# V rows of a scan step from 128-row products, and new cost estimates for a planner

## The chip, the cores and the metric

The kernel runs on one core of a Trainium2 chip. The time is the device time of one execution in microseconds, and the median of the runs is what is compared. TensorE (PE) does the matrix products, VectorE (DVE) and ScalarE (ACT) the elementwise work, GpSimd (POOL) a little of it, and SyncE (SP) issues the DMA transfers, in the order of its queue.

## The reference

One layer of a hybrid model on 512 latent and 128 context tokens of width 1024. Cut to what matters here:

```python
def _wkv(s0, r, w, k, v, a, b, reverse):
    def step(S, inp):
        rt, wt, kt, vt, at, bt = inp
        sa = jnp.einsum('bhvk,bhk->bhv', S, at)
        S = S * wt[:, :, None, :] + sa[..., None] * bt[:, :, None, :] + vt[..., None] * kt[:, :, None, :]
        return S, jnp.einsum('bhvk,bhk->bhv', S, rt)
    s_fin, ys = lax.scan(step, s0, xs, reverse=reverse)

def _layer(x, cond, s0_f, s0_b, rows, lp):
    mod = jax.nn.silu(cond) @ lp['ada_w'] + lp['ada_b']
    sh1, sc1, g1, sh2, sc2, g2 = jnp.split(mod[:, None, :], 6, axis=-1)
    xn = _rmsnorm(x, lp['norm1_g']) * (1 + sc1) + sh1
    proj = xn @ lp['w_in']                      # r, k, v, GLU input, two gates
    y_r, s_f, s_b = _rwkv_branch(xn, rkv, s0_f, s0_b, lp)   # _wkv in both directions, 8 heads of 64
    y_c = _conv_branch(glu_in, rows, lp)
    merged = jax.nn.sigmoid(gate_r) * y_r + jax.nn.sigmoid(gate_c) * y_c
    x = x + g1 * (merged @ lp['w_o'])
    xn2 = _rmsnorm(x, lp['norm2_g']) * (1 + sc2) + sh2
    x = x + g2 * (jnp.square(jax.nn.relu(xn2 @ lp['mlp_w1'])) @ lp['mlp_w2'])
```

All is computed in float32.

## The kernel before

Channels lie on the 128 partitions and the 640 tokens in the free dimension. A dense product in full precision is made of three products of split operands (`mm3`), 24 instructions of 128x128 by 320 columns for each half of four weight tiles. The kernel has three stages. First come the norm, the first 16 column blocks of the modulation `mod` and the low-rank products (to about 60 us). Then, to about 780 us, runs a mixed stage: the input projections, the scan, the convolution, the gates and the merge. Then follow the output projection and the MLP, dense work alone.

The scan works in chunks of 32 tokens. A head pair `p` (four of them, two heads `s` each, two directions `d`) has its own operands, its triangular solve (`solve`, with `gram`, `inverse` and `fold`) and its chain of 20 steps (`chain`). A step multiplies the state and the V rows, which lie stacked in the tile `svu`, by the chunk's operands. The V rows enter PSUM through `values`: four small products (two heads, two directions) with a part of an identity matrix move 32 tokens of V to the partitions where the chain needs them. `vS` holds V and `vr` holds V in reversed order. ACT then copies the sum of V rows and state products (the `ps` products of the step) into `svu`.

The order of PE, DVE and ACT in the mixed stage is written out by the program itself. Generators ("lanes") issue their instructions and yield: a number is a wait in planned us, a bare `yield` means to go on when the last issued instruction is done, by the plan, plus `SEM` (0.2), and a letter names an engine that has to be nearly free. The main loop takes the most urgent lane that is ready (`URGENT`), and fills PE with dense products where none is. The planned time `now` moves with PE's products (`mm`), and the functions `cost_v`, `cost_a` and `cost_g` estimate the other engines. `mm` also keeps an account of columns: a float32 product adds its cycles, times its rows / 128, times 0.5; the account drains with planned time at `QUOTA * ENTRY / TICK`, and while it is low (`hungry`) dense products go first. A wait that the plan does not know of, say for a transfer or for a PSUM bank, stands in PE's queue for real, and all products behind it wait too. SP's queue is not written out in this way.

The lane `ada_all` makes the other 32 column blocks of `mod`, which are read only behind the mixed stage. For each it waits `GAP_ADA`, then `ada` loads the first half of the weights (256 KB) into `adl`, which has one buffer, and issues its four products; waits 2.5; loads the second half into the same buffer, and issues four more. The loads come out of a generator (`adl_load`), so each is issued by the program right ahead of its products; SP may run it as soon as the buffer is read and all that stands before it in SP's queue is out.

`operands(p)` ends with two DVE operations on `kk`, whose result `bonus(p)` multiplies on PE. `inverse(p)` uses three DVE transposes of 128x1024. `root` raises a small tile to a power on GpSimd.

Of the kernel before, what the change touches and what calls it, by code (L numbers as in the profile page):

```python
# [13 lines left out]
ALU = mybir.AluOpType  # L14
# [46 lines left out]
LEAD, SEM, LOAD = 0.40, 0.2, 4.0  # L61
# [1 line left out]

URGENT = dict(scan=0, split=0.3, shift=1.45, post=1, side=0.9, solve=1, prep=1.5, lora=2, ada=4, out=4.5, branch=0.5, conv=1.6)

GAP_LORA, GAP_ADA = 1.5, 3.5
V_STEP = 20
GLU_AT = 12
TICK, ENTRY, QUOTA, CREDIT, STAY, DEBT = 3.413, 3060, 1.55, 700, 350, 6000
# [7 lines left out]
def hybrid_step(ctx: ExitStack, tc: tile.TileContext, I, O):  # L77
# [32 lines left out]
    def aps_(kw, *names):  # L110
        return sum(hasattr(kw.get(k), "shape") for k in names)

    def cost_v(name, n, src, kw):
        return 0.07 + 0.06 * aps_(kw, "scalar", "scalar1") + n / (480 if name == "tensor_tensor_scan" else 960)

    def cost_a(name, n, src, kw):
        return (0.08 if src[0].space == PSUM else 0.16) + 0.093 * aps_(kw, "scale", "bias") + n / 1400

    def cost_g(name, n, src, kw):
        return 1.9 if kw.get("op") == ALU.pow else 0.26 + n / (450 if name == "tensor_tensor" else 960)  # L120

    V, A, G = Timed(nc.vector, "V", cost_v), Timed(nc.scalar, "A", cost_a), Timed(nc.gpsimd, "G", cost_g)

    def advance(t):
        dt, now[0] = max(t - now[0], 0.0), max(now[0], t)
        gated["credit"] = max(gated["credit"] - QUOTA * ENTRY / TICK * dt, -DEBT)
        while now[0] >= gated["end"]:
            gated.update(cols=0.0, end=gated["end"] + TICK, warm=gated["cols"] >= ENTRY)

    def bank(tag="mm"):  # L130
        return pp.tile([P, 512], F32, name="ps_" + tag, tag=tag, bufs=2 if tag == "mm" else 1)
# [10 lines left out]
    def ldtmp():  # L142
        pool, n, cols = tmp_pool[-1]
        return pool.tile([P, cols], F32, name="tmp", tag="tmp", bufs=n)
# [10 lines left out]
    ident = cst[:, CST_ID:CST_ID + 128]  # L155
# [36 lines left out]
    def mm(out, lhsT, rhs, start=True, stop=True, **kw):  # L192
        PE.matmul(out=out, lhsT=lhsT, rhs=rhs, start=start, stop=stop, **kw)  # L193
        cyc = math.prod(rhs.shape[1:]) * (1 if rhs.dtype == F32R else 2 if "is_transpose" in kw else 4)
        m = math.prod(lhsT.shape[1:])
        overlap = 128 // m if m < 128 else 128 // rhs.shape[0]
        cols = cyc * rhs.shape[0] / 128 * (1 if rhs.dtype == F32R else 0.5)
        gated["cols"] += cols
        gated["burst"] -= cols
        gated["credit"] = min(gated["credit"] + cols, CREDIT)  # L200
        kind = (m, rhs.shape[0], rhs.dtype)
        if kind != gated["kind"]:
            advance(now[0] + SWITCH * gated["drain"] / (2400 if gated["warm"] else 1200))
        gated.update(kind=kind, drain=0 if rhs.dtype == F32R else max(cyc, 256) - max(cyc / overlap, 64))
        advance(now[0] + (max(cyc / overlap, 64) + EXTRA) / (2400 if gated["warm"] else 1200))
        ready[out.name] = ("P", now[0] + SEM / 2)
        last[0] = now[0]
# [7 lines left out]
    planner, calm = [lambda: None], []  # L215
# [167 lines left out]
    def ada(cols, tag, raws):  # L383

        n = len(cols) * P
        ps = bank(tag)
        for k0, k1, raw in raws:
            for k in range(k0, k1):
                g = 32 * (k % 4)
                mm(ps[g:g + 32, 0:n], csb[:, 2 * k:2 * k + 32], raw[:, k - k0, :], k < 4, k >= 4, tile_position=(0, g))  # L390
            yield 2.5 if k0 == 0 else 0.0
        e = ldtmp()[:, 0:n]
        A.activation(e, ps[:, 0:n], AF.Copy)
        yield
        for i, col in enumerate(cols):
            mm(ps[:, n + 2 * i:n + 2 * i + 2], e[:, i * P:(i + 1) * P], sel)
        for i, col in enumerate(cols):
            A.activation(mod[:, col, :], ps[:, n + 2 * i:n + 2 * i + 2], AF.Identity, bias=pc("ada_b", col))
# [52 lines left out]
    for k in range(KD):  # L451
        q = sut([P, T], "sq", 2) if k else sums
# [3 lines left out]
    ps = bank("t")  # L456
# [5 lines left out]
    for tag, a, b in (("a0", 0, 4), ("b0", 4, 5)):  # L462
        ps = bank(tag)
# [90 lines left out]
    rk, grp, shifting = {}, {}, []  # L554
# [107 lines left out]
    def operands(p):  # L662

        gr = grp[p]
        gr["Dc"] = wt([P, NY], "Dc", 2)
        r, k = rk[0, p], rk[1, p]

        def load(d):
            th, at = st([P, T], "tA"), st([P, T], f"ath{d}")
            DMA.dma_start(out=th, in_=dram(f"z0{d}{p}"))  # L670
            DMA.dma_start(out=at, in_=dram(f"z1{d}{p}"))
            return th, at

        loaded = load(0)
        t0 = st([P, T], "pt0")
        A.activation(t0, k, AF.Square, scale=pc("k_k", p))
        kk = gr["kk"] = st([P, T], "kk")
        yield
        yield from inv_norm(t0, 1.0, "max", 1e-24, ("t",) * 3,
                            lambda a, b, ps: V.scalar_tensor_tensor(out=kk[:, a:b], in0=k[:, a:b], scalar=pc("k_k", p),  # L680
                                                                    in1=ps, op0=ALU.mult, op1=ALU.mult))
        ath = []
        for d in range(2):
            ys = slice(20 * d, 20 * d + 20)

            def tv(ap):
                return (ap[:, ::-1] if d else ap).rearrange("p (y t) -> p y t", t=C32)


            th, at = loaded  # L690
            ath.append(at)
            A.activation(th, th, AF.Copy, bias=1.0)
            yield "T"
            cs = st([P, 20, C32], "tB")
            csf = cs.rearrange("p y t -> p (y t)")
            for a, b in HALVES:
                V.tensor_tensor_scan(out=csf[:, a:b], data0=smask, data1=th[:, a:b], initial=0.0,
                                     op0=ALU.mult, op1=ALU.add)
                yield "V"
            if d == 0:  # L700
                loaded = load(1)
            yield "T"
            A.activation(E[:, :, 1:33], cs, AF.Exp, scale=-0.5 * CDEC)
            yield "A"
            A.activation(cs, cs, AF.Exp, scale=0.5 * CDEC)
            yield "A"
            if d == 0:
                while p and (3 not in rates or (p > 1 and p - 2 not in chained)):
                    yield 0.2
                ARGH = gr["ARGH"] = st([P, 2, NY, 64], "ARGH", 2)  # L710
            A.activation(gr["Dc"][:, ys].unsqueeze(2), E[:, :, 32:33], AF.Copy)
            V.tensor_tensor(out=ARGH[:, 0, ys, 0:32], in0=tv(kk), in1=E[:, :, 0:32], op=ALU.mult)
            yield "V"
            V.tensor_tensor(out=ARGH[:, 0, ys, 32:64], in0=tv(r), in1=E[:, :, 1:33], op=ALU.mult)
            DMA.dma_start(out=ARGH[64:128, 1, ys, :], in_=ARGH[64:128, 0, ys, :])
            yield "V"
            if d == 0:
                while p and turned[p - 1] < 3:
                    yield 0.2
                BK = gr["BK"] = wt([P, NY, 64], "BK")  # L720
            bc, kc = (0, 32) if d == 0 else (32, 0)
            t1 = st([P, T], "pt0")
            V.scalar_tensor_tensor(out=t1, in0=at, scalar=1.0, in1=kk, op0=ALU.add, op1=ALU.mult)
            yield "V"
            V.scalar_tensor_tensor(out=BK[:, ys, bc:bc + 32], in0=tv(t1), scalar=-0.5, in1=cs,
                                   op0=ALU.mult, op1=ALU.mult)
            yield "A"
            A.activation(at, at, AF.Identity, scale=ka2[:, p:p + 1], bias=ka2[:, 4 + p:5 + p])
            yield "T"
            V.tensor_tensor(out=at, in0=at, in1=k, op=ALU.mult)  # L730
            yield "V"
            V.tensor_tensor(out=BK[:, ys, kc:kc + 32], in0=tv(at), in1=cs, op=ALU.mult)
            yield "V"
        operated.add(p)
        V.tensor_tensor(out=kk, in0=ath[0], in1=ath[1], op=ALU.add)
        yield "V"
        V.scalar_tensor_tensor(out=kk, in0=kk, scalar=pc("r_k", p), in1=r, op0=ALU.mult, op1=ALU.mult)
        yield SEM

    BKt = wt([P, 2, NY, 64], "BKt")  # L740
    for s in range(2):
# [3 lines left out]
    vr = wt([P, T], "vr")  # L745
# [14 lines left out]
    def vq(s, d):  # L760
        return 32 * (2 * (1 - s) + 1 - d)
# [218 lines left out]
    def cidx(c, i):  # L980

        return (i, 4 + i) if c == "l" else (16 + i, i)

    STEPS = [("c", i) for i in range(4)] + [("l", i) for i in range(16)]

    def values(p, n):

        S, ps = SVU[n % 2], grp[p]["ps"]
        for s, d in UNITS:
            lo, q, t = 64 * s, vq(s, d), 32 * cidx(*STEPS[n])[d]  # L990
            mm(ps[q:q + 32, d, :], (vr if d else rk[2, p])[lo:lo + 64, t:t + 32], ident[lo:lo + 64, lo:lo + 64],
               tile_position=(lo, q))
        for s in range(2):
            o = slice(64 - 64 * s, 128 - 64 * s)
            A.activation(S[o, :, s, :], ps[o], AF.Copy)
# [654 lines left out]
```

## Time and profile before

| | us |
|---|---|
| median of 3 runs | 1296.28 |
| lowest and highest | 1286.36, 1297.65 |
| profiled execution | 1300.42 |
| its span, first to last instruction | 1298.6 |

In the profiled execution PE is busy for 95% of the span, DVE for 56%, ACT for 42% and GpSimd for 12%; PE's mean granted clock is 0.958 of its full 2.4 GHz. The times of busy PE are modelled, as matmuls are pipelined, so the start-to-start distance of two groups says more than a duration. A wait is put down to what came last before the engine went on.

### The profile page before, as it was taken

To read this page: it belongs to the slowest core of one execution; us is meant where nothing else is said; L and a number is where in the kernel's file an instruction comes from. 1 tells how busy PE (TensorE), PEld (TensorE's weight loads), DVE (VectorE), ACT (ScalarE), POOL (GpSimd) and SP (SyncE) were. 2 spreads that over 40 slices of the span, in tenths; PEclk is the share of its full clock that TensorE was granted. 3 is DMA by queue.
4 is the path that set the end of the run, shared out by engine and by line. 5 is a ranking of instruction groups with operands and counts; after the bars stand their busy time and mean duration, and the time that the engine had idled before them with its cause. 6 is when DMAs were issued, how large, how long until landed. Compare 5 with 4: busy or idle time off the path is not lost.

```text
span 1298.6 us, 31716 instructions
## 1 busy us (share of the span) xinstructions
PE 1228.2 (95%) x13362; PEld 1092.9 (84%) x13362; DVE 720.9 (56%) x1446; ACT 548.8 (42%) x1390; POOL 152.4 (12%) x112
## 2 busy tenths in 40 slices
PE   8988899998999899999979999999999999999996
PEld 5776676777677776777979999999999999999996
DVE  5525576747557766877953365664433443444344
ACT  5545466634555565465225123354421431342130
POOL 1122120112011100122413310000000000000000
PEclk9998999968799989999989999999999999999998
DMA  9445433113222522343413853112222222222222
GB/s 370 151 158 175 143 109 114 59 43 119 77 94 68 153 92 70 116 126 93 136 58 121 270 195 125 49 50 82 72 75 81 67 82 74 74 82 69 78 74 82
DMA packets 82575, 140.43 MB, mean 108 GB/s; under 512 B 17024, under 2 KB 31616, under 8 KB 82432
## 3 DMA queue, kind: packets, MB, share of 16 engines
q1 hardware_dynamic: 82432, 138.39, 33.2%
q8 instruction: 105, 1.72, 0.6%
q14 instruction: 38, 0.31, 0.1%
HBM read 113.52 MB, written 22.22 MB: 105 GB/s over the span
## 4 chain that ended last, share of the span: by engine, by line
PE 82%; DVE 7%; DMA 6%; issue 2%; ACT 1%; SPq 0%; POOL 0%; POOLq 0%; DVEq 0%; ACTq 0%
PE ps_mm L193 43%; PE ps_b L193 24%; PE ps_t L193 7%; PE ps_a L193 6%; DMA adl_w<-in_adal 3%; PE ps_ad L193 3%; DVE BK_w L106 2%; DVE cacc_w L106 1%; DMA adar_s<-in_adaw 1%; DVE vS_w L106 1%; DVE ARGH_t L106 1%; DMA u_t<-gate 1%; DMA svu_w<-in_st 0%; DVE kk_t L106 0%; DVE svu_w L106 0%
## 5 line engine op out<-in xcount | busy, mean ns | idle before, releaser
L193 PE MATMUL ps_mm<-xh_t,wh_t 128*128 128x320 f32 x584 | 198.2, 339 | 0.9 <-ACT tmp L106 0.9
L193 PE MATMUL ps_mm<-xh_t,wl_t 128*128 128x320 f32 x584 | 198.8, 340 | 0.0
L193 PE MATMUL ps_mm<-xl_t,wh_t 128*128 128x320 f32 x584 | 196.7, 337 | 0.0
L106 ACT ACTIVATE wh_t<-wr_t 128x512 fp32r<-128x512 f32 x135 | 84.9, 629 | 143.2 <-PE ps_b L193 108.4
L106 POOL TENSOR_TENSOR wl_t<-wr_t,wh_t 128x512 fp32r<-128x512 f32 x63 | 85.0, 1350 | 462.0 <-ACT wh_t L106 418.0
L106 ACT ACTIVATE svu_w<-ps_a 64x128 f32<-64x128 f32 x320 | 87.0, 272 | 122.9 <-PE ps_a L193 117.3
L193 PEld LDWEIGHTS ps_mm<-xh_t,wl_t 128*128 128x128 f32 x584 | 117.0, 200 | 10.8 <-issue 7.2
L193 PEld LDWEIGHTS ps_mm<-xl_t,wh_t 128*128 128x128 f32 x584 | 116.7, 200 | 9.6 <-issue 6.1
L193 PEld LDWEIGHTS ps_mm<-xh_t,wh_t 128*128 128x128 f32 x584 | 116.3, 199 | 9.6 <-issue 4.3
L106 DVE SCALAR_TENSOR_TENSOR cacc_w<-upad_w,par_t,cacc_w 128x640 f32<-128x640 f32 x90 | 88.6, 984 | 4.3 <-ACT cacc_w L106 2.1
L106 DVE TENSOR_TENSOR wl_t<-wr_t,wh_t 128x512 fp32r<-128x512 f32 x72 | 49.7, 690 | 56.2 <-ACT wh_t L106 56.2
L106 ACT ACTIVATE tmp<-ps_mm 128x320 f32<-128x320 f32 x80 | 34.9, 436 | 98.9 <-PE ps_mm L193 90.4
L193 PE MATMUL ps_mm<-ARGH_t,wh_t 128*128 128x320 f32 x284 | 74.8, 308 | 0.0
L106 DVE TENSOR_TENSOR svu_w<-ps_b,Dc_w 64x128 f32<-64x128 f32 x152 | 43.7, 288 | 54.5 <-PE ps_b L193 51.0
L106 POOL TENSOR_TENSOR rt_t<-rt_t,mhalf_t 128x3 f32<-128x3 f32 (+1 forms) x7 | 6.5, 921 | 532.0 <-DVE rt_t L106 532.0
L193 PE MATMUL ps_mm<-ARGH_t,wl_t 128*128 128x320 f32 x212 | 65.8, 310 | 0.0
L106 ACT ACTIVATE mwh<-wr_t 128x512 fp32r<-128x512 f32 x49 | 31.0, 632 | 71.1 <-PE ps_b L193 66.8
L106 DVE SCALAR_TENSOR_TENSOR ARGH_t<-ps_mm,mod_t,ARGH_t 128x320 f32<-128x320 f32 (+2 forms) x45 | 22.6, 511 | 59.9 <-PE ps_mm L193 59.9
L106 DVE TENSOR_TENSOR tmp<-tmp 128x320 f32<-128x320 f32 x64 | 31.2, 489 | 43.8 <-ACT tmp L106 43.7
L106 DVE TENSOR_TENSOR mwl<-wr_t,mwh 128x512 fp32r<-128x512 f32 x49 | 33.8, 690 | 34.9 <-ACT mwh L106 34.9
L193 PEld LDWEIGHTS ps_mm<-ARGH_t,wh_t 128*128 128x128 f32 x284 | 50.4, 188 | 0.0
L106 ACT ACTIVATE BKt_w<-ps_a 32x512 f32<-32x512 f32 (+3 forms) x80 | 39.9, 503 | 19.9 <-PE ps_a L193 18.9
(372 smaller groups left out, 3226.2 us busy)
## 6 DMA issues: line engine op xcount, KB each, us to landing
wr_t<-in_w SPq DMA_DIRECT2D x214, 256.0 KB, 2.7
adl_w<-in_adal SPq DMA_DIRECT2D x64, 256.0 KB, 3.0
adar_s<-in_adaw SPq DMA_DIRECT2D x16, 512.0 KB, 8.4
ARGH_t<-in_x SPq DMA_DIRECT2D x8, 640.0 KB, 6.9
z<-tmp SPq DMA_DIRECT2D x32, 160.0 KB, 3.0
gate<-tmp SPq DMA_DIRECT2D x32, 160.0 KB, 2.2
tA_t<-z SPq DMA_DIRECT2D x8, 320.0 KB, 3.1
ath_t<-z SPq DMA_DIRECT2D x8, 320.0 KB, 3.3
```

Of the source, the lines that this page charges most:

```text
L106: return f(*args, **kw)
L193: PE.matmul(out=out, lhsT=lhsT, rhs=rhs, start=start, stop=stop, **kw)
```

## The change

The products of `values` read all 128 rows of V, with the 64 columns of the 128x128 identity that pick the head, in place of 64 rows with a 64x64 identity. They are the same four a step, with the same results. Five estimates of the plan are changed: the wait ahead of a modulation column (`GAP_ADA`) and between its halves, the cost of a DVE transpose, the cost of the power on GpSimd, and the end of `operands`, which now goes on when its last operation is done by the plan and not 0.2 us later.

```diff
-GAP_LORA, GAP_ADA = 1.5, 3.5
+GAP_LORA, GAP_ADA = 1.5, 4.5
     def cost_v(name, n, src, kw):
-        return 0.07 + 0.06 * aps_(kw, "scalar", "scalar1") + n / (480 if name == "tensor_tensor_scan" else 960)
+        return 0.07 + 0.06 * aps_(kw, "scalar", "scalar1") + n / (480 if name == "tensor_tensor_scan" else 520 if name == "transpose" else 960)
     def cost_g(name, n, src, kw):
-        return 1.9 if kw.get("op") == ALU.pow else 0.26 + n / (450 if name == "tensor_tensor" else 960)
+        return 2.6 if kw.get("op") == ALU.pow else 0.26 + n / (450 if name == "tensor_tensor" else 960)
     def ada(cols, tag, raws):
-            yield 2.5 if k0 == 0 else 0.0
+            yield (GAP_ADA if calm else 2.5) if k0 == 0 else 0.0
     def operands(p):
         V.scalar_tensor_tensor(out=kk, in0=kk, scalar=pc("r_k", p), in1=r, op0=ALU.mult, op1=ALU.mult)
-        yield SEM
+        yield
     def values(p, n):
         for s, d in UNITS:
-            lo, q, t = 64 * s, vq(s, d), 32 * cidx(*STEPS[n])[d]
-            mm(ps[q:q + 32, d, :], (vr if d else rk[2, p])[lo:lo + 64, t:t + 32], ident[lo:lo + 64, lo:lo + 64],
-               tile_position=(lo, q))
+            q, t = vq(s, d), 32 * cidx(*STEPS[n])[d]
+            mm(ps[q:q + 32, d, :], (vr if d else rk[2, p])[:, t:t + 32], ident[:, 64 * s:64 * s + 64], tile_position=(0, q))
```

`calm` is set in the mixed stage.

## Rows read from the trace of the kernel before

**Rows 1.** The page's part 2: granted clock in tenths, 40 slices

```profile
PEclk9998999968799989999989999999999999999998
```

**Rows 2.** Windows: stretch, length, busy PE, PEld, DVE, ACT, POOL, clock, DMA, GB/s

```profile
60.00:780.00 720.00, 667.41 (x9535) 549.52 (x9532) 448.46 (x886) 352.40 (x995) 140.45 (x99) 0.93 0.38 119
780.00:1298.60 518.60, 505.65 (x3452) 504.74 (x3450) 238.01 (x482) 165.27 (x323) 3.40 (x4) 0.99 0.24 76
```

**Rows 3.** Waits of PE: who waited for whom, us in total, times, longest

```profile
PE ps_ad L193 <- DMA adl_w<-in_adal: 17.0, 9, 2.9
PE ps_t L193 <- DVE kk_t L106: 7.5, 8, 1.8
...
PE ps_mm L193 <- DVE BK_w L106: 5.7, 2, 5.2
```

**Rows 4.** Timeline of PE, one step: start, us, operation, tile, count

```profile
448.21 0.32 PE L193 MATMUL ps_a<-svu_w,ARGH_t 128*32 128x64 f32 x8
448.46 0.43 PE L193 MATMUL ps_t<-ARGH_t,svu_w 128*64 128x32 f32 x8
...
449.66 0.45 PE L193 MATMUL ps_b<-svu_w,BKt_w 128*64 128x64 f32 x8
450.04 0.25 PE L193 MATMUL ps_a<-cst_t,vS_w 64*32 64x64 f32 x2
...
450.28 0.41 PE L193 MATMUL ps_mm<-xl_t,wh_t 128*128 128x320 f32 x1
```

**Rows 5.** Tile adl_w: products (ns min/median/max, first and last start), transfers' landing

```profile
L193 PE MATMUL ps_ad<-adl_w,csb_t x512: 272/297/423, 59.7 to 552.3; 128*32 128x128 f32 x171
...
DMA to landing us min/median/max: 2.5/3.0/5.0
```

**Rows 6.** Timeline of PE: the waits for adl_w over 2 us

```profile
64.72 0.43 PE L193 MATMUL ps_ad<-adl_w,csb_t 128*32 128x128 f32 x8 [2.07 <-DMA adl_w<-in_adal]
...
77.62 0.65 PE L193 MATMUL ps_ad<-adl_w,csb_t 128*32 128x128 f32 x8 [2.55 <-DMA adl_w<-in_adal]
...
112.01 0.65 PE L193 MATMUL ps_ad<-adl_w,csb_t 128*32 128x128 f32 x8 [2.29 <-DMA adl_w<-in_adal]
...
328.03 0.66 PE L193 MATMUL ps_ad<-adl_w,csb_t 128*32 128x128 f32 x8 [2.88 <-DMA adl_w<-in_adal]
...
454.82 0.43 PE L193 MATMUL ps_ad<-adl_w,csb_t 128*32 128x128 f32 x8 [2.02 <-DMA adl_w<-in_adal]
```

**Rows 7.** Timeline of PE and of SP's queue, 321 to 325 us

```profile
321.29 0.43 PE L193 MATMUL ps_ad<-adl_w,csb_t 128*32 128x128 f32 x8
...
324.21 0.32 SPq L670 DMA_DIRECT2D tA_t<-z  x1
324.64 4.44 SPq L620 DMA_DIRECT2D adl_w<-in_adal  x2
```

**Rows 8.** Windows of four stretches with a low granted clock

```profile
108.00:126.00 18.00, 15.05 (x79) 12.16 (x76) 10.68 (x15) 8.90 (x19) 2.77 (x2) 0.72 0.48 143
324.00:348.00 24.00, 21.12 (x309) 16.32 (x313) 10.80 (x24) 10.73 (x34) 2.60 (x2) 0.64 0.30 86
456.00:468.00 12.00, 12.00 (x228) 10.02 (x228) 8.18 (x17) 7.18 (x19) 0.00 (x0) 0.72 0.25 78
258.00:288.00 30.00, 28.02 (x319) 20.85 (x316) 14.34 (x55) 10.64 (x27) 4.50 (x3) 0.60 0.12 37
```

**Rows 9.** Groups by line and form: busy us, mean ns, idle before

```profile
L106 DVE STREAM_TRANSPOSE Gt_w<-Gf_w 128x1024 f32<-128x1024 f32 x4 | 7.8, 1951 | 0.0
...
L106 POOL TENSOR_TENSOR rh_t<-rh_t,mhalf_t 128x10 f32<-128x10 f32 x8 | 17.3, 2162 | 37.0 <-DVE rh_t L106 19.8 <-DVE Nb_w L106 14.6 <-PE ps_ad L193 2.6
```

**Rows 10.** Timeline of PE and DVE: two waits for kk_t

```profile
134.38 0.76 PE L193 MATMUL ps_t<-kk_t,cst_t 128*64 128x320 f32 x4 [1.14 <-DVE kk_t L106]
...
495.04 1.89 DVE L106 STREAM_TRANSPOSE Gt_w<-Gf_w 128x1024 f32<-128x1024 f32 x1
...
497.35 1.24 PE L193 MATMUL ps_t<-kk_t,cst_t 128*64 128x320 f32 x4 [1.79 <-DVE kk_t L106]
```

## The prediction

> **What bounds the kernel now.** I read the page's clock row first. TensorE (PE below) is granted nearly its full clock, except in some slices between the fourth and the twenty-first of 40 [rows 1]. Then the windows: the stretch 60 to 780 us, in which a planner mixes the scan with the projections, has PE busy for 667.4 of 720 us at a mean granted clock of 0.93; from 780 us on it is busy for 505.7 of 518.6 at 0.99 [rows 2]. The change touches nothing behind 780 us, so all that can move lies in the first stretch. There PE is the engine whose queue the time follows: 52.6 us of it idle, and 0.07 x 720 = 50 us lost to the lower of its two clock levels (1.2 instead of 2.4 GHz). What PE waited for stands in the list of waits: the loads of `adl_w` come first with 17.0 us in nine waits, the longest 2.9, then `kk_t` with 7.5 us in eight, and one wait of 5.2 for `BK_w` [rows 3]. So the kernel is bound by PE's fixed work plus the places where the plan put a product ahead of its operand. A corrected estimate is worth such a wait, and what the clock loses behind it.
>
> **The V products.** They come four to a step, in 20 steps of 4 head pairs: 80 steps. The edit puts no instruction in and takes none out; each product reads 128 rows where it read 64. Before, the V products of a step start at 450.04 and the next work at 450.28: 0.24 us. The trace holds the new shape too: the first products of the same step, 128 rows by 32 columns with 64 columns moving, start at 448.21 and the next work at 448.46: 0.25 us [rows 4]. So I take 80 x 0.01 = 0.8 us lost, rounded to nothing. The products before the V products use 128 rows and 64 columns and start 0.38 us ahead of them [rows 4]; since the column count still changes there, I see no time saved at that border.
>
> The Trainium skill, "TensorEngine Tiling (Array Packing)", section "Theoretical Speedup", speaks against the edit: a contraction of 64 or less may gain up to a factor of two by row tiling, which the edit gives up. By it the sum would be worse by 80 x 0.24 = 19 us, an estimate that takes the duration from the trace. The rows side against it here: the 128-row group takes as long as the 64-row group [rows 4], since four column strips already serve all four products.
>
> The second effect is on the plan. Its account books a product by its rows: a V product goes from 64 to 128 columns, a step from 256 to 512. A richer account asks for less dense work between steps. The code's rate is 1.55 x 3060 / 3.413 = 1390 columns per us, so 256 more buy 0.18 us a step, 15 us over the 80 steps, in which other small work can come earlier. That moves work, and removes none; I price it at nothing and keep its danger as a rival.
>
> **The waits for the modulation weights.** This is the largest term. Each of 32 columns comes in two halves through one buffer. The gap that the plan leaves between the halves' products goes from 2.5 to 4.5 us, the one before the first half from 3.5 to 4.5. A load takes 3.0 us at the median, and 2.5 to 5.0, from issue to landing [rows 5]; 2.5 us could not hold it, and where it went well the plan had other work there. Five waits are longer than 2 us [rows 6]; each of them, and each of the other four, stands at a second half. With two more us for each, 0.07 + 0.55 + 0.29 + 0.88 + 0.02 = 1.8 us would be left of 17.0, so at best 15.2 go. At worst none go: the load stands in SP's queue, and that queue runs in order. At 321.29 the first half was read, but its buffer's next load started only at 324.64, right behind a load of `tA_t` at 324.21 that had waited for VectorE (DVE) [rows 7]. Two more us of plan put more transfers ahead of it. I take 11, nearer the best: the usual issue and load (0.5 + 3.0) fit into 4.5 with one us to spare, which they did not before.
>
> The longer gaps add at most 32 x 3 = 96 us to this lane. Its last product starts at 552.3 [rows 5]; 648 is still well ahead of 780, where the values are read, and PE's other work covers it. Were that cover gone, each column left over would cost its two gaps, 9 us.
>
> **The clock behind these waits.** Three stretches that begin with such a wait have granted clocks of 0.72 (108 to 126), 0.64 (324 to 348) and 0.72 (456 to 468) [rows 8]: 18 x 0.28 + 24 x 0.36 + 12 x 0.28 = 17.0 us lost. The bounds are 0 and 17.0. In each, PE was idle for 2.0 to 2.9 us, and then stayed at the low level for long after [rows 6, 8]. But 258 to 288 has 0.60 too [rows 8], with no such wait ahead of it: a wait is not the only cause, and a moved order may fall into others. I take half, 8.5.
>
> **The other estimates.** DVE's transposes are planned at 1.14 us and measure 1.95 in the form shown; the new 2.04 is near it. The power on GpSimd is planned at 1.9 and measures 2.16; the new 2.6 leaves room [rows 9]. At 497.35 PE waited 1.79 us for a DVE result that was queued behind a transpose of 1.89, and at 134.38 it waited 1.14 for `kk_t`, whose producer the changed last `yield` of `operands` now waits for [rows 10]. No long wait of PE's ends at the power: it gets nothing. Bounds 0 and 2.9; I take 2. The other waits for `kk_t` and the 5.2 us for `BK_w` [rows 3] are for PSUM banks and for the convolution on DVE, whose estimate is not changed; they stay.
>
> **Sum.** 0 + 11 + 8.5 + 2 = 21.5 us. The profiled execution took 1300.42 us, its span is 1298.6; 1300.4 - 21.5 = 1279. It lies 4 us above the median of the runs shown, 1296.28, whose spread (1286.36 to 1297.65) is as wide as one of the low stretches above.
>
> **Rivals.**
> (a) The forecast: most waits for `adl_w` go, half of the clock comes back. 1279, its own range 1266 to 1291. Chance 0.50.
> (b) The change doesn't do what it says: the second load still stands behind a waiting transfer. For it speaks the row at 324.21 [rows 7]; against it, that nine waits stand against 64 loads [rows 3, 5]. A quarter of 15.2, and the 2 us: 1300.4 - 5.8 = 1295. Chance 0.25.
> (c) Slower. The plan believes the V products keep the array twice as active, puts fewer dense products between steps, and the clock does not follow. The place is the scans; the price is that of 258 to 288, 30 x 0.40 = 12.0 us [rows 8], which lies in the scan of the first head pair. One more in each of three scans is 36 us against 21.5 saved: 1315. It decides from two on (24 us). For it: that stretch fell to the low level without a long wait. Against it: the plan moves by 0.18 us a step only. The Trainium skill, "TensorE: Matmul & The Clock Gate", section "What's actually happening", supports it: the clock goes by how busy PE has been, and by that alone more rows would earn nothing. No row here separates rows from time. Chance 0.12.
> (d) All of it goes: 15.2 + 17.0 + 2.9 = 35.1, 1265. For it, that the low stretches start at the waits; against it, 258 to 288. Chance 0.10.
> (e) The 128-row products no longer overlap: 19 us of the 21.5 are lost, 1298. Rows 4 speak against it. Chance 0.03.
>
> **How the numbers follow.** About 1% (13 us) is what a measurement of this kernel can tell from no change, so faster means below 1283.3 and slower above 1309.2. Faster: 0.41 of (a), 0.10 of (d), 0.04 of (b): 0.55. Same: 0.09 of (a), 0.19 of (b), 0.02 of (c), 0.03 of (e): 0.33. Slower: 0.10 of (c) and 0.02 of (b): 0.12. The range goes from 1254, below (d), to 1306: outside it are most of (c) and the tails of (b) and (d), some 0.17.
>
> **What would show it.** In the list of PE's waits, `adl_w` at 2 to 6 us instead of 17.0, and its longest below 1.5; the V products as `128*32` with the next work 0.25 us later; last `adl_w` product between 580 and 650; the windows 60 to 780 ending some 20 us earlier at a clock of 0.94 to 0.95; the stretch behind unchanged within 3 us. If `adl_w` still has over 10 us, (b) holds and the time is near 1295. If it is gone but the mean clock over the scans is lower than 0.93, (c) holds. If the V groups take 0.4 us or more, (e). I would be wrong altogether if a new wait of many us showed up, on an operand that the old order never touched early.

## The result, and the profile after

The changed kernel takes 1256.43 us, the median of four runs (1256.1 to 1257.99); the kernel before, on the same chip, 1293.99 (1286.36 to 1297.65). The ratio is 0.972, with a 95% interval of 0.967 to 0.977: faster, by 37.6 us. The profiled execution took 1256.1 us against 1300.42, so 44.3 less, with a span of 1254.3. Executions of one kernel differ with the clock that they are granted: the ratios leave out those more than 1.5% above the fastest of their kernel, and the profiled execution of before is itself one of the slow ones, 6.4 us above its median. The forecast was 1279; the time lies in its range, 2 us above the lower end, and on its side, but the gain is 1.7 times (by the medians) to 2.1 times (by the profiled executions) the 21.5 us of the sum.

The clock row of the page after (tenths, 40 slices) has three slices below 9 ahead of its last, none under 8, where that of before had six, down to 6 [rows 1]:

```profile
PEclk8999999999999999999989999899999999999998
```

The windows after, cut at the end of the mixed stage, which is the first addition of the output projection into the residual: stretch, length, busy PE, PEld, DVE, ACT, POOL, clock, DMA share, GB/s.

```profile
60.00:733.74 673.74, 640.52 (x9560) 526.84 (x9559) 449.90 (x892) 353.93 (x1000) 145.12 (x101) 0.99 0.42 128
733.74:1254.30 520.56, 507.49 (x3453) 506.57 (x3451) 238.54 (x484) 164.90 (x323) 3.40 (x4) 0.99 0.24 76
```

In the kernel before the same cut falls at 779.37 us, with 666.78 us of busy PE in 719.37 at a clock of 0.93 (the stretch of [rows 2] less its last 0.6 us):

```profile
60.00:779.37 719.37, 666.78 (x9531) 548.89 (x9528) 447.91 (x885) 352.40 (x995) 140.45 (x99) 0.93 0.38 119
```

The stage is 45.6 us shorter. What follows it takes 1254.3 - 733.7 = 520.6 us where it took 1298.6 - 779.4 = 519.2, so all of the gain lies in the mixed stage. There PE's idle time fell from 719.4 - 666.8 = 52.6 us to 673.7 - 640.5 = 33.2. The clock's loss, (1 - mean clock) x length, fell from 0.07 x 719.4 = 50.4 us to 0.01 x 673.7 = 6.7 (the clock has two digits, so each may be off by 3.5 us). PE's busy time fell by 26.3 us although its instructions are the same in number: that goes with the clock, as the fit below shows over all kernels.

The waits of PE after (who waited for whom, us in total, times, longest) have the loads of `adl_w` far down with 0.6 us, where they came first [rows 3], and no `BK_w`:

```profile
PE ps_t L193 <- DVE kk_t L106: 7.2, 10, 1.0
PE ps_t L193 <- DVE vS_w L106: 7.1, 8, 1.7
PE ps_a L193 <- DVE svu_w L106: 3.5, 7, 1.1
...
PE ps_ad L193 <- DMA adl_w<-in_adal: 0.6, 2, 0.4
```

Tile `adl_w` after, as in [rows 5]: the loads take as long as before, at the median, and the lane ends 84 us later.

```profile
L193 PE MATMUL ps_ad<-adl_w,csb_t x512: 269/273/423, 65.2 to 636.6; 128*32 128x128 f32 x171
...
DMA to landing us min/median/max: 2.5/3.0/6.3
```

The timeline of PE at one step after, as in [rows 4]: the V products read 128 rows and the next work starts 205.02 - 204.77 = 0.25 us behind them.

```profile
204.39 0.45 PE L193 MATMUL ps_b<-svu_w,BKt_w 128*64 128x64 f32 x8
204.77 0.25 PE L193 MATMUL ps_a<-cst_t,vS_w 128*32 128x64 f32 x2
205.02 0.41 PE L193 MATMUL ps_mm<-xl_t,wh_t 128*128 128x320 f32 x1
```

### The profile page after: what moved, and what is told of

Its sections match the earlier page's. It is cut to its first block, busy times and chain, and to the rows that moved or that the text cites. A ratio compares the mean times of both kernels' runs of the same rounds, so it can differ in the third digit from the quotient of the medians.

```text
span 1254.3 us, 31727 instructions
## 1 busy us (share of the span) xinstructions
PE 1202.9 (96%) x13362; PEld 1072.2 (85%) x13362; DVE 721.3 (58%) x1446; ACT 547.4 (44%) x1390; POOL 154.9 (12%) x112
## 4 chain that ended last, share of the span: by engine, by line
PE 83%; DVE 8%; DMA 4%; issue 2%; ACT 2%; SPq 0%; POOL 0%; POOLq 0%; DVEq 0%; ACTq 0%
PE ps_mm L193 44%; PE ps_b L193 24%; PE ps_t L193 6%; PE ps_a L193 6%; PE ps_ad L193 2%; DVE cacc_w L106 1%; DVE ARGH_t L106 1%; DVE BK_w L106 1%; DVE kk_t L106 1%; DMA g<-tmp 1%; DVE vS_w L106 1%; DVE Gt_w L106 1%; DMA adl_w<-in_adal 1%; DVE prod_w L106 1%; ACT tmp L106 0%
## 5 line engine op out<-in xcount | busy, mean ns | idle before, releaser
L106 ACT ACTIVATE wh_t<-wr_t 128x512 fp32r<-128x512 f32 x140 | 87.9, 628 | 135.2 <-PE ps_b L193 106.5
L106 POOL TENSOR_TENSOR wl_t<-wr_t,wh_t 128x512 fp32r<-128x512 f32 x68 | 94.0, 1383 | 417.7 <-ACT wh_t L106 368.2
L106 DVE TENSOR_TENSOR svu_w<-ps_b,Dc_w 64x128 f32<-64x128 f32 x152 | 43.7, 287 | 31.9 <-PE ps_b L193 27.5
L106 DVE SCALAR_TENSOR_TENSOR ARGH_t<-ps_mm,mod_t,ARGH_t 128x320 f32<-128x320 f32 (+2 forms) x45 | 22.6, 512 | 59.6 <-PE ps_mm L193 59.6
L106 DVE TENSOR_TENSOR tmp<-tmp 128x320 f32<-128x320 f32 x64 | 31.1, 489 | 42.5 <-ACT tmp L106 42.3
```

Source lines behind the costliest of these rows:

```text
L106: return f(*args, **kw)
```

## The experiments

The change has three kinds of parts: the V products (on the chip, and in the plan's account), the two gaps of the `adl_w` lane, and the three other estimates. Theory 1: the time follows PE's idle time and the clock's loss in the mixed stage, and a part is worth the waits that it removes. Rival 2: the V products themselves, by what they do to the array or to its clock. Rival 3: each edit moves the written-out order, and the order by itself scatters the time, whatever the edit means. This table has the runs; "idle" and "clock loss" are worked out from one window from 60 us to the end of the mixed stage, as above, in the profiled execution of each.

| kernel | median us | ratio to before [95%] | profiled us | `adl_w` waits | idle | clock loss |
|---|---|---|---|---|---|---|
| before | 1293.99 | 1 | 1300.42 | 17.0 in 9 | 52.6 | 50.4 |
| after | 1256.43 | 0.972 [0.967, 0.977] | 1256.1 | 0.6 in 2 | 33.2 | 6.7 |
| e1 V rows, plan of before | 1291.13 | 1.003 [0.998, 1.007] | 1282.9 | 14.8 in 8 | 52.0 | 28.0 |
| e2 after, V on 64 rows | 1252.19 | 0.970 [0.963, 0.977] | 1257.5 | none | 32.1 | 13.5 |
| e3 gaps alone | 1279.40 | 0.992 [0.987, 0.997] | 1284.3 | 0.6 in 1 | 39.1 | 42.3 |
| e4 V edit alone | 1271.96 | 0.984 [0.975, 0.992] | 1268.1 | 13.2 in 9 | 38.0 | 20.6 |
| e5 three estimates alone | 1270.14 | 0.982 [0.975, 0.989] | | | | |
| e5b the same | 1258.26 | 0.972 [0.962, 0.983] | 1263.1 | 6.8 in 6 | 34.8 | 20.4 |
| e6 after, old gaps | 1272.68 | 0.986 [0.979, 0.993] | 1269.0 | 9.6 in 9 | 37.5 | 20.6 |
| e8 after, old V edit | 1255.17 | 0.971 [0.965, 0.977] | 1250.9 | 0.5 in 1 | 31.2 | 6.7 |
| e14 gaps and V edit | 1257.31 | 0.975 [0.969, 0.981] | 1262.6 | 0.4 in 2 | 33.2 | 27.3 |
| e9 after, 8 loads doubled | 1256.02 | 0.972 [0.966, 0.979] | 1256.4 | 5.7 in 2 | 36.0 | 13.5 |
| e13 after, 8 loads tripled | 1285.18 | 0.997 [0.993, 1.000] | 1283.2 | 22.6 in 7 | 53.2 | 28.0 |
| e10 before, V booked as 96 | 1289.07 | 0.996 [0.991, 1.001] | 1296.7 | 18.6 in 9 | 52.0 | 42.9 |
| e17 before, V booked as 160 | 1278.55 | 0.990 [0.981, 0.999] | 1275.9 | 13.5 in 7 | 47.5 | 20.7 |
| e15 before, LEAD 0.42 | 1280.95 | 0.993 [0.988, 0.997] | 1282.2 | 17.4 in 11 | 46.6 | 28.0 |
| e16 after, one more estimate | 1261.85 | 0.975 [0.968, 0.981] | 1260.2 | 3.5 in 1 | 34.3 | 13.5 |
| e20 after, LEAD 0.38 | 1265.37 | 0.976 [0.969, 0.983] | 1266.5 | 0.5 in 2 | 41.7 | 13.7 |
| e18 after, LEAD 0.42 | 1241.35 | 0.959 [0.953, 0.965] | 1244.0 | 1.7 in 1 | 28.8 | 6.6 |
| e19 after, LEAD 0.44 | 1279.49 | 0.988 [0.981, 0.994] | 1280.6 | none | 37.4 | 42.0 |

A least-squares fit over the 19 profiled executions gives time = 1217 + 0.94 x idle + 0.69 x clock loss, with a residual of 2.3 us. Part of this is bookkeeping: the stage is as long as its busy and its idle time together, and what follows it stays between 517.8 and 522.5 us. What the fit shows is that the busy time of the stage follows the clock loss alone (632 + 0.69 x loss, residual 2.5 us), so no kernel here gains more than that in a third way. Theory 1's first half holds for every kernel here, and the question is what moves the two terms.

### The V products on the chip

`book` is a new argument of `mm` that sets the rows which the plan sees, in its account and where it asks whether one product has the form of the last, in place of `rhs.shape[0]`. With it the chip runs the one form and the plan sees the other, and the order of all engines stays that of before (e1) or that of after (e2).

```diff
 e1: before, and in values:
+            mm(ps[q:q + 32, d, :], (vr if d else rk[2, p])[:, t:t + 32], ident[:, 64 * s:64 * s + 64],
+               book=64, tile_position=(0, q))
 e2: after, and in values:
+            mm(ps[q:q + 32, d, :], (vr if d else rk[2, p])[lo:lo + 64, t:t + 32], ident[lo:lo + 64, lo:lo + 64],
+               book=128, tile_position=(lo, q))
```

e1: 

> The kernel before, with the V products on 128 rows, but booked in the plan's account as 64 rows, so that every engine runs the very order of before. Theory 1 (the wider V products themselves keep the clock up): the low stretch 258 to 288 us and those behind the waits for adl_w shrink, the mean clock of 60 to 780 us rises from 0.93 to 0.97 or more, and the time falls by 20 to 30 us to some 1268. Theory 2 (the waits for adl_w pull the clock down; the rows earn nothing): waits for adl_w near 17 us, the same low stretches, the time within 5 us of before.

e2: 

> The kernel after, with the V products on 64 rows, but booked as 128, so that the order on all engines is that of after. Theory 1 (rows count): low stretches come back in the scans, mean clock of the mixed stage about 0.95, time 1275 to 1285. Theory 2 (the gaps did it): clock as in after, 0.98 to 0.99 in the mixed stage, 1255 to 1259.

Measured: 1.003 for e1 and 0.970 for e2, against 1 and 0.972. On either order the products are worth nothing, and rival 2 falls. e1 shows one more thing. Its order is that of before, and yet its clock loss is 28.0 and not 50.4 us. The kernel before ran the end of the first scan, 258 to 288, at 0.60 [rows 8]; in e1 the same products of PE run from 253.62 to 274.31, at 1.00:

```profile
253.62:274.31 20.69, 18.72 (x320) 14.35 (x317) 13.82 (x52) 10.47 (x27) 4.49 (x3) 1.00 0.17 53
```

So the same work in the same order took 20.7 us in one execution and 30 in the other. The rows are not what decides: at 310 to 330, around one of the waits for `adl_w`, e1 is low as well.

```profile
310.00:330.00 20.00, 16.69 (x193) 12.82 (x193) 8.58 (x17) 8.04 (x28) 2.60 (x2) 0.57 0.27 72
```

It is a draw: the ten executions of e1 run from 1280.24 to 1297.9 us, with a ratio of 1.003 to before, and the one that was profiled, 1282.88, is among the shortest.

### One part alone

```diff
 e3: before, and
-GAP_LORA, GAP_ADA = 1.5, 3.5
+GAP_LORA, GAP_ADA = 1.5, 4.5
-            yield 2.5 if k0 == 0 else 0.0
+            yield (GAP_ADA if calm else 2.5) if k0 == 0 else 0.0
 e4: before, and the four lines of the V edit in values
 e5, e5b: before, and cost_v (transpose), cost_g (power) and the last yield of operands as in after
```

e3: 

> The kernel before with the two longer gaps of the modulation weights alone. Theory 1: waits for adl_w fall from 17 to below 3 us, the stretches behind them mostly go, those in the scans (like 258 to 288) stay; time 1270 to 1280. Theory 2: the waits go and all the low stretches with them, 1255 to 1265. If the order of before was merely unlucky, the time may lie anywhere in between, with new waits.

e4: 

> The kernel before with the 128-row V products as the change has them, booked as 128, and the old estimates. Theory 1: as for the wider products in the old order, some 20 us below before, waits for adl_w still 10 us or more, 1265 to 1278. Theory 2: no gain, or a loss, since the plan puts less dense work between the steps: 1290 to 1310.

e5: 

> The kernel before with the three other estimates alone (transpose, power, end of operands). Theory (the waits of PE set the time, and each that is gone takes clock with it): the waits for kk_t of 1.1 and 1.8 us go, those for adl_w stay near 15 us; 1283 to 1294. Rival (the order alone decides, any edit of the plan gains): 1260 to 1275, with the waits for adl_w still there.

e5b: 

> The three other estimates alone, once more, for a usable trace: their time of 1270 stood 20 us below before where 2 were foreseen. Theory A (right estimates): the waits of 1.4 us and more for DVE results behind transposes are gone, those for adl_w are still near 15 us, clock about 0.96; 1264 to 1276. Theory B (another order): other waits are gone as well, such as the 5.2 us for BK_w.

The one profiled execution of e5 took 2763.82 us, more than twice its other three (1265.88 to 1270.35), and is left aside; e5b is the same kernel again.

e3 takes the waits for `adl_w` from 17.0 to 0.6 us and gains 0.8% [0.3, 1.3], some 11 us. Its windows and its waits of PE:

```profile
60.00:764.72 704.72, 665.58 (x9563) 545.95 (x9562) 446.73 (x892) 355.15 (x1001) 141.06 (x99) 0.94 0.39 122
```

```profile
PE ps_t L193 <- DVE kk_t L106: 8.9, 9, 2.1
...
PE ps_t L193 <- issue: 4.2, 3, 2.5
PE ps_t L193 <- DVE Y_w L106: 3.0, 2, 2.5
```

The idle time fell by 13.5 us, but the clock rose no further than to 0.94: in the new order PE waits 2.1 us for `kk_t` and 2.5 for `Y_w` at other places, and behind the latter (at 239.7) the clock is low again:

```profile
240.00:272.00 32.00, 30.49 (x325) 22.71 (x321) 11.44 (x51) 9.92 (x30) 1.95 (x1) 0.52 0.10 34
```

e4 is the surprise: the V edit alone gains 1.6%, though its products are worth nothing on the chip. So it is the booking that moves the order. Its windows, and its wait for `adl_w`:

```profile
60.00:748.27 688.27, 650.29 (x9562) 532.22 (x9562) 446.27 (x893) 355.11 (x1001) 141.06 (x99) 0.97 0.40 125
```

```profile
PE ps_ad L193 <- DMA adl_w<-in_adal: 13.2, 9, 2.7
```

Most of the waits for the loads are there; of the 14.6 us of idle time that have gone, 10.8 lay elsewhere, the 5.2 us for `BK_w` among them, and the clock came to 0.97. The three estimates alone gain as much, 1.8% and 2.8%.

### After, less one part

```diff
 e6: after, and
-GAP_LORA, GAP_ADA = 1.5, 4.5
+GAP_LORA, GAP_ADA = 1.5, 3.5
-            yield (GAP_ADA if calm else 2.5) if k0 == 0 else 0.0
+            yield 2.5 if k0 == 0 else 0.0
 e8: after, with values of before
 e14: before, with the edits of e3 and of e4
```

e6: 

> The kernel after with the two gaps of the modulation weights as before (3.5 and 2.5). Theory: waits for adl_w come back at 12 to 17 us and with them low stretches; 1268 to 1280. Rival: the gain came from the order, not from these waits: 1254 to 1262.

e8: 

> The kernel after without the edit of the V products, on the chip and in the account: gaps and other estimates alone. If the three parts add up, the V edit's share of some 20 us is missing: 1270 to 1282. If the V edit matters only by shuffling the order, it may lie anywhere from 1255 to 1285, and the trace shows which waits stand in for it.

e14: 

> The kernel before with the gaps and the V edit, without the three other estimates. If the estimates of transpose, power and operands carry the second half of the gain: some 1270 to 1280, with waits for DVE results behind transposes of 1.4 to 2.5 us. If the V edit can stand in for them: 1254 to 1262.

Without the new gaps (e6) 16 us of the gain are lost; without the V edit (e8) nothing is, and without the estimates (e14) nothing that can be told, at 1257.31. So the parts don't add up: e3, e4 and e5 gain 0.8, 1.6 and 1.8 to 2.8%, together 4.2 to 5.2, and the whole gains 2.8. The gaps are worth something beside each of the others (e4 to e14 0.9%, e6 to after 1.4%, e5 and e5b to e8 1.1% and 0.1%); the booking and the estimates do the same job twice, or are two draws from one pot.

### Late loads

```diff
 e9 (e13): after, and in adl_load
-            DMA.dma_start(out=raw, in_=I["adal"][col - 16, :, 4 * j:4 * j + 4, :])
+            [DMA.dma_start(out=raw, in_=I["adal"][col - 16, :, 4 * j:4 * j + 4, :])
+             for _ in range(2 if j and col % 4 == 0 else 1)]                   # e13: 3
```

e9: 

> The kernel after, in which the second half of every fourth modulation column is loaded twice over, one transfer behind the other, in the same order on PE, DVE, ACT and GpSimd. Eight waits of PE of 1 to 2.5 us for adl_w come back, 8 to 20 us in all. Theory (a wait pulls the clock down, and costs about twice its length): mean clock of the mixed stage falls from 0.99 to 0.95 or 0.97, time 1275 to 1290. Rival (a wait costs itself): clock stays at 0.98 or more, time 1262 to 1272.

e13: 

> The kernel after, in which the second half of every fourth modulation column is loaded three times over, one transfer behind the other (some 9.5 us, against 5.4 to 14.9 us between the halves' products), in the same order on PE, DVE, ACT and GpSimd. Six to eight waits of PE of 1 to 4 us, 12 to 22 us in all. Theory (a wait pulls the clock down, and costs up to twice its length): mean clock of the mixed stage 0.94 to 0.97, time 1275 to 1295. Rival (a wait costs at most itself, and later slack may take it up): clock 0.98 or more, time 1258 to 1274.

Eight waits were expected of e9 and two came, 5.7 us in all: in the order of after most halves stand far enough apart to hide a second load. The time, 1256.02, didn't move, though its interval is 8 us wide to either side. With three loads (e13) seven waits came, 22.6 us in all and 5.7 the longest, and the time rose by 1285.18 - 1256.43 = 28.8 us, with no instruction of the compute engines moved. The windows of e13 (the stage, and the 8 us behind one of the seven waits), the sum of these waits, and that one in PE's timeline:

```profile
60.00:761.23 701.23, 648.08 (x9542) 532.61 (x9541) 446.94 (x886) 351.78 (x996) 141.31 (x99) 0.96 0.42 128
456.00:464.00 8.00, 7.93 (x74) 6.01 (x74) 3.44 (x7) 3.34 (x11) 0.00 (x0) 0.59 0.17 56
```

```profile
PE ps_ad L193 <- DMA adl_w<-in_adal: 22.6, 7, 5.7
```

```profile
456.07 0.65 PE L193 MATMUL ps_ad<-adl_w,csb_t 128*32 128x128 f32 x8 [2.85 <-DMA adl_w<-in_adal]
```

After starts the same products at 440.61 and runs the 8 us behind them at full clock:

```profile
440.61:448.61 8.00, 8.00 (x111) 6.25 (x107) 6.96 (x13) 5.63 (x23) 1.32 (x1) 1.00 0.19 62
```

In the 8 us behind a wait of 2.85 PE gets through 74 products in place of 111. Over the stage the 22 us of waits more brought 19.9 us more of idle time and 21 us more of clock loss. In e9 and e13 nothing but the loads differs from after, so e13 prices such a wait: 28.8 / 22 = 1.3 times its length by the medians, 1.2 by the profiled executions (27.1 us), 1.5 by the ratios to before (0.025 x 1294 = 32 us). It is not a price for every order: e3 lost 16.4 us of these waits and gained 11.

### The order by itself

```diff
 e10 (e17): before, and in values
-               tile_position=(lo, q))
+               book=96, tile_position=(lo, q))                                # e17: 160
 e15, e18 (e20, e19): before, and after, with
-LEAD, SEM, LOAD = 0.40, 0.2, 4.0
+LEAD, SEM, LOAD = 0.42, 0.2, 4.0                                              # e20: 0.38, e19: 0.44
```

`LEAD` is how long ahead of an engine's planned end a lane that waits for that engine may go on. A hundredth or two of a us has no meaning of its own; it moves the order.

e10: 

> The kernel before, with the V products as they were on the chip, booked as 96 rows: half of the V edit's step in the plan's account, and nothing else. Theory A (a richer account helps by itself): about half of the 22 us that the full booking gave, 1280 to 1286. Theory B (the order of before is an unlucky one, and any shift of the plan loses its long waits): as much as the full booking or an unsystematic amount, 1265 to 1300, with the list of PE's waits telling which.

e17: 

> The kernel before, V products unchanged on the chip, booked as 160 rows, beyond the 128 of the V edit (22 us) and the 96 that gave 4 us. Theory A (a richer account helps): 1262 to 1272. Theory B (order by chance): anywhere from 1262 to 1292, not in line with the two others.

e15: 

> The kernel before with one constant of the plan moved by a twentieth (LEAD 0.42 instead of 0.40), which corrects nothing and only reorders. Theory A (each estimate in the change gains because it is right): within 8 us of before, 1284 to 1302. Theory B (before is an unlucky order): 1262 to 1283, waits for DVE of 1.8 us and more gone by chance, those for adl_w still near 15 us.

e18: 

> The kernel after with LEAD 0.42 instead of 0.40, the shift that took 12 us off before without correcting anything. Theory A (after has few long waits because its estimates are right, whatever the order): within 6 us of 1256, waits for adl_w below 3 us. Theory B (after is a lucky order): 1262 to 1280 with new long waits.

e19: 

> The kernel after with LEAD 0.44. The value 0.42 gave 1241, 15 us below after. Theory A (a larger LEAD is the better one): 1235 to 1246. Theory B (each value is another order, all with right estimates): 1240 to 1262, in no line with 0.40 and 0.42, waits for adl_w below 5 us in any case.

e20: 

> The kernel after with LEAD 0.38. Theory A (a larger LEAD is the better one): 1258 to 1275. Theory B (each value is another order): 1240 to 1262, waits for adl_w below 5 us.

If a richer account were a good in itself, a half dose would give half. The V rows booked as 64, 96, 128 and 160 give a ratio of 1, 0.996, 0.984 and 0.990: no straight dose, and the neutral shift of e15 gains 0.7% [0.3, 1.2] too. On the kernel after, `LEAD` at 0.38, 0.40, 0.42 and 0.44 gives 1265, 1256, 1241 and 1279 us: 38 us between neighbours. The windows of e18 and e19:

```profile
60.00:721.81 661.81, 633.03 (x9549) 521.40 (x9549) 443.65 (x885) 354.15 (x997) 141.26 (x99) 0.99 0.42 129
```

```profile
60.00:759.30 699.30, 661.88 (x9535) 542.81 (x9534) 438.16 (x886) 352.74 (x995) 140.46 (x98) 0.94 0.39 122
```

e19 has 8.6 us more of idle time and 35 us more of clock loss, and no wait for `adl_w`: rival 3 holds. Taken as two families, the kernels with the old gaps (before, e4, e5 with e5b as one, e6, e10, e15, e17) have a mean ratio of 0.989 with a spread (one standard deviation) of 0.008, those with the new gaps (after, e3, e8, e14, e16, e18, e19, e20) 0.976 and 0.010. So an order moves the time by 10 to 13 us whichever edit made it (the spreads hold the noise of the ratios too). The means differ by 0.0135 or 17 us, with a standard error of 6, but that is not the gaps alone: of the eight new kernels five have the V edit and the estimates as well, of the seven old ones only e6.

e18 beats both kernels at 1241.35 us, 0.959 [0.953, 0.965]. It was found, not reasoned: its neighbours are worse.

### A further estimate

The plan prices DVE's three-operand operations on 640 columns too low; e16 adds the difference.

```diff
 e16: after, and in cost_v
-        return 0.07 + 0.06 * aps_(kw, "scalar", "scalar1") + n / (480 if name == "tensor_tensor_scan" else 520 if name == "transpose" else 960)
+        return 0.07 + 0.06 * aps_(kw, "scalar", "scalar1") + (0.19 if name == "scalar_tensor_tensor" and n == 640 else 0) + n / (480 if name == "tensor_tensor_scan" else 520 if name == "transpose" else 960)
```

> The kernel after with one more estimate corrected: DVE's three-operand operation on 640 columns, planned at 0.80 us and measured at 0.98, gets 0.19 more. Theory A (each right estimate gains): waits for DVE results (svu_w, BK_w, rS_w) shrink, 1248 to 1255. Theory B: nothing left to gain there, 1253 to 1262.

1261.85 us, 0.975 [0.968, 0.981]: no gain, perhaps 5 us lost. A truer estimate isn't by itself a faster order.

## Why the prediction was right or wrong, point by point

**The V products.** Right: 0.25 us a group, and 1.003 [0.998, 1.007] with the order held. The Trainium skill, "TensorEngine Tiling (Array Packing)", section "Theoretical Speedup", gives up to a factor of two for a contraction of 64 or less; e1 and e2 don't show it, as the timeline of before had said [rows 4]. Rival (e) falls.

**The plan's account.** Priced at nothing, its danger kept as rival (c): on the order of before the booking moves the time by 22 us (e4), down and not up as (c) had it; on top of the rest it moves nothing (e8). "That moves work, and removes none" is true, and yet a moved order is worth or costs 10 to 13 us here, a term with no sign that the sum left out.

**The waits for `adl_w`.** 11 us were taken out of bounds of 0 to 15.2; 16.4 of 17.0 went. The lane ended at 636.6, within the 580 to 650 named. Rival (b), the load stuck in SP's queue, falls: the longest landing even rose to 6.3 us, but no product stood at its end.

**The clock.** The term that was mis-sized. The text itself worked out 50 us of clock loss in the stage, but bounded the gain by the 17.0 of three stretches that begin with a wait for `adl_w`, and took half, 8.5. Between the two profiled executions the loss fell by 50.4 - 6.7 = 43.7 us, worth 0.69 x 43.7 = 30 by the fit. A part of that is the draw: e1, in the same order, lost 28.0 where the profiled execution of before lost 50.4. Every execution has its span and mean clock on record; over the whole span, (1 - clock) x span has a median of 42.6 us in the 50 executions of before that count in the ratios of the experiments, and of 20.7 in the four of after. These 22 us are worth 15 to 18, at the 0.69 of the fit or the 0.81 of the last section: twice the 8.5, and as much as the upper bound. The step that failed is to take half of the loss of three stretches that were chosen by the waits ahead of them: 33 of the 50 us lay in others, which the upper bound left out. They could go because the other long waits go with the order: `BK_w`, 5.2 us, said to stay, is absent in after, e3, e4 and e6, and back with 2.8 in e8.

**The other estimates.** 2 us were taken out of bounds of 0 to 2.9. The waits for `kk_t` went from 7.5 to 7.2 in all, the longest from 1.8 to 1.0: the direct effect was no larger than foreseen. But e5 and e5b gain 23 to 36 us by the order that these estimates make. As with the booking, the bound was that of the waits at hand.

**The sum, measured.** Idle time 19.4 x 0.94 = 18 us, where the waits and the estimates were forecast at 13; clock 15 to 18, where 8.5 was forecast; together 33 to 36, against 37.6 between the medians. With the 30 us of the profiled pair it is 48, against 44.3 there.

**What it is due to.** Shown: the products themselves give nothing, so the gain comes from the plan; the longer gaps leave 3.5 us or less of the waits for `adl_w` in every order that has them, with the loads as they are. The rest comes with the order, and how it divides is not shown. The table has all eight combinations of gaps, V edit and estimates (before, e3, e4, e5 with e5b, e14, e8, e6, after). The gaps are worth 12 us over the four pairs that differ in them alone (11, 12, 8 and 18), the V edit 8 over its four, the estimates 14; by the scatter of the orders, about 0.009, each of these means has a standard error of 8, so none is clear of it. The whole change is: before and its neighbours (e10, e15, e17) have a mean ratio of 0.995, after and its own (e16, e18, e19, e20) 0.974, which is 27 us with a standard error of 7. About 10 of the 37.6 us are then the luck of this pair, before being 7 us above its neighbourhood's mean and after 2 below. With the gaps in place the V edit or the estimates alone still gain (e3 to e14 1.7%, e3 to e8 2.1%), and the second of the two adds nothing. Whether a richer account and truer estimates make good orders on the whole, or were lucky draws, stays open; it would take some ten neutral shifts of each to tell.

**The rivals and the range.** (a)'s mechanism is there for the waits, at the wrong size for the clock. In size the gain is that of (d), "all of it goes", which had a chance of 0.10: 35.1 us, against 37.6. That its time, 1265, is 9 us too high is mostly the start of the sum, 1300.4, which lies above the median; and not all that went had been on its list (`BK_w`). (c), slower by a cooler array, falls: the mean clock of the stage is 0.99.

## What to carry to other kernels

Price a wait of the busiest engine by its length and by the clock that falls behind it, 1.2 to 1.5 times its length in e13, and bound the gain by the whole clock loss of the stage, not by the stretches whose cause you know. Where a program writes its own order, any edit of an estimate is a new draw: hold the order (let the plan see the old form) to measure the operation, and run a few neutral shifts to learn the scatter, before a gain or a loss of its size is put down to what the edit means. Of the waits, remove first those for loads through one buffer: of the eight orders with the longer gaps seven had under 2 us of them.

## What the hardware showed that had not been expected

The granted clock is not a function of the order alone. In the profiled execution of before 11 of 13 waits of PE of 1.3 us or more in the mixed stage were followed within about 2 us by a fall to the low level; in e1, with the same order, 6 of 12, and before ranged from 1277.66 to 1317.85 us over 19 runs beside e1. After, with no wait of over 1.7 us, ranged over 1.9 us in four runs. The Trainium skill, "TensorE: Matmul & The Clock Gate", section "What's actually happening", says that the point at which the clock changes varies from run to run, since the chip's look at activity runs freely against the kernel; these runs vary too, in falls in the middle of the kernel, and by 22 us of clock loss between two executions of one order; no run here shows the reason.

The lower level also costs less than its name: by the fit over the kernels a us of clock loss is worth 0.69 us of time, and over 50 executions of before alone, by their spans and mean clocks, 0.81 (1277.66 to 1305.19 us, residual 1.5 us). That would fit work that does not follow the clock, such as PE's waits inside a low stretch; that was not tested.
